# RWKV-7 waves: alpha and key-times-a kept in DRAM, y normalised on ScalarE, two steps of the scores' order exchanged

## The chip, the cores and the metric

The kernel runs on one core of a Trainium2 chip. The metric is the time of one execution on the device in microseconds (us). The engines are named as in the profile: PE is TensorE (PEld its weight loads), DVE is VectorE, ACT is ScalarE, POOL is GpSimd, SP is SyncE, which here issues every DMA.

## The reference

One inference step of a two-layer trunk, layer 0 gated DeltaNet, layer 1 RWKV-7, on 1024 + 16 prompt rows and 8 sequences of 8 sample rows, 1024 wide. Only the RWKV layer is touched. Per head (16 heads of 64) and per row t it computes, with the vectors r, k, v, the decay d and the gate a:

```python
kk = l2norm((k * k_k).reshape(B, T, H, N))
k = k * (1.0 + (a - 1.0) * k_a)
decay = jnp.exp(-jnp.exp(w))
b_h = kk * a_h
def step(S, inp):
    S = (S * d_t[:, :, None, :]
         + jnp.einsum('bhvk,bhk->bhv', S, -kk_t)[..., None] * b_t[:, :, None, :]
         + v_t[..., None] * k_t[:, :, None, :])
    return S, jnp.einsum('bhvk,bhk->bhv', S, r_t)
...
y = (y - mean) * lax.rsqrt(var + GN_EPS) * lnx_w.reshape(H, N) + lnx_b.reshape(H, N)
y = y + jnp.sum(r_h * k_h * r_k, -1, keepdims=True) * v_h
y = y.reshape(B, T, D) * jax.nn.silu(z)
return y @ w_o, S, xn[:, -1]
```

## The kernel before

The rows are cut into three segments of 384, 384 and 336 and the heads into eight pairs, so there are 24 tiles "pair of heads x segment" of [128 features, 384 rows]. Each tile has six chunks of 64 rows. The kernel computes the recurrence in its chunked form: alpha is kk times the decay up to the row before, the keys times a are divided by the decay (kk * a * iD), and inside a chunk the rank-one updates need the inverse of a triangular matrix.

The RWKV layer has three stages. First the projections for k, with decay and a (`keys_decay_rate`), which write their results to DRAM (`csd`, `kd`, `ad`). Second the projections for r, v and part of the gate z. Between these, `rwkv_inverse` works through the 24 tiles in five groups: `rwkv_keys` makes kk, Dp (decay) and iD (its inverse), `alpha` makes the alpha tile `sal`, two products make the tile kk * a * iD, PE multiplies them, and the inverses go to DRAM as `ttd`. Third `wave`: it walks through 58 waves (tau from -3 to 54). A tile takes two waves to enter, six waves to run through its chunks, and is finished some waves later; three tiles are in flight at a time. In this stage the order on PE is as written in the program (`manual_schedule`); the other engines' queues, and all of them before this stage, are ordered by the framework's scheduler, which simulates the program. Blocks under `high_priority` go first there, and `issue_after` keeps a wave's other work behind its inner step.

In a wave `step_solve` multiplies the scores G with the ring UV (values above, solved rows below) and the alpha half of AR with the state; ACT copies the result to X; `step_inner` multiplies with the inverse TT; ACT writes the solved rows back into UV; then fillers run (output projections, the gate), and `step_state` updates states and y. Around this, for each tile:

- `rwkv_front` loads cs, k, a, r and v from DRAM, and makes kk, Dp, iD, AR (alpha and r times decay), k2 and BK (the two keys over the decay). It makes alpha and kk * a * iD a second time, on POOL.
- Six parts follow in two waves, three in each, as `P.parts` lists them: `scores(0)` and `scores(3)` (each takes both PSUM banks of the tag "f", which DVE empties into G), `bonus`, `values` (three transposes; ACT copies them into the ring), `keys(0)` and `keys(3)` (three transposes each; ACT copies them into BT), and `system` (the load of TT). A wave runs its first part between solve and inner step, its second before `step_state`, its third after it.
- `rwkv_finish` takes mean and variance of y on DVE, the power on POOL, three steps of refinement on DVE, and normalises six tiles of 128x64 on POOL (L1551); PE transposes them in a later wave, and the bonus and the gate follow.

## Time and profile before

| | |
|---|---|
| median of 3 runs | 2374.34 us (2370.59 to 2375.54) |
| profiled execution | 2374.91 us, its span 2373.2 us |
| instructions | 54463 |
| first and last inner step of the waves | 1876.0 and 2327.2 us after the span's start |
| mean granted PE clock | 0.967 |

Lines of the profile give a start in us, a duration in us, engine, line, operation and tiles; a bracket holds the idle time of that engine just before, and what ended it. "x6" counts merged instructions. A group's row has busy us and mean ns of one instruction, then the idle time before.

### The profile page before, as it was taken

The numbers are of one execution on the slowest core, as the hardware profiler recorded it, in microseconds if no ns is written. First come the engines' busy times: TensorE is split into PE (matmuls) and PEld (weight loads), VectorE is DVE, ScalarE is ACT, GpSimd is POOL, SyncE is SP. The second block draws the span as 40 slices with busy tenths as digits, with TensorE's granted clock in tenths as the row PEclk, the third lists the DMA queues.
The fourth block names the chain that finished last, engine by engine and source line by source line (L and its number), as shares of the span: only waits on it lengthen the run. The fifth ranks groups of instructions, "written<-read, shape, count | busy, mean of one in ns | idle before, by whom it ended". The sixth has DMA issues, their size and how long they took to land. (4 is left out here: it accounts for less than half of the span.)

```text
span 2373.2 us, 54463 instructions
## 1 busy us (share of the span) xinstructions
PE 2168.7 (91%) x19737; PEld 1962.9 (83%) x19737; DVE 1617.0 (68%) x4195; ACT 1248.0 (53%) x3479; POOL 1113.8 (47%) x1566
## 2 busy tenths in 40 slices
PE   5989999999999999999989998998999888888886
PEld 5888989888898989898989998987878776777775
DVE  6868677685858686873346724389896666778754
ACT  5455655554656555566243646555453454556552
POOL 3435343343444353433223513355454666777764
PEclk9999999999999999999999999999999999999998
DMA  3323332324233333435262245566754544555543
GB/s 113 106 74 104 87 102 78 96 71 113 68 105 94 85 98 88 115 107 163 62 165 76 72 156 173 143 164 165 188 135 129 178 115 141 158 178 182 178 138 125
DMA packets 470535, 290.01 MB, mean 122 GB/s; under 512 B 188121, under 2 KB 455642, under 8 KB 470266
## 3 DMA queue, kind: packets, MB, share of 16 engines
q1 hardware_dynamic: 470266, 286.53, 42.7%
q8 instruction: 156, 2.56, 0.5%
q14 instruction: 113, 0.93, 0.1%
HBM read 200.53 MB, written 85.89 MB: 121 GB/s over the span
## 5 line engine op out<-in xcount | busy, mean ns | idle before, releaser
L90 POOL TENSOR_TENSOR wlo<-wraw,whi 128x512 fp32r<-128x512 f32 (+2 forms) x252 | 329.7, 1311 | 349.2 <-ACT whi L86 323.2
L76 PE MATMUL d<-xc,whi 128*128 128x384 f32 (+2 forms) x910 | 259.1, 341 | 4.8 <-POOL xc L90 2.8
L86 ACT CAST whi<-wraw 128x512 fp32r<-128x512 f32 (+2 forms) x252 | 151.6, 603 | 130.6 <-PE dq L76 50.5
L419 DVE SCALAR_TENSOR_TENSOR cvy<-raw,cw,cvy 128x408 f32<-128x408 f32 (+2 forms) x288 | 178.9, 634 | 17.6 <-ACT cvy L62 15.7
L452 DVE TENSOR_TENSOR invtmp<-invA,invT 72x31 f32<-72x31 f32 (+31 forms) x403 | 170.4, 423 | 13.0 <-DMA invA<-ltd 5.1
L76 PEld LDWEIGHTS d<-xc,whi 128*128 128x128 f32 (+1 forms) x910 | 167.8, 191 | 12.6 <-issue 5.3
L454 DVE TENSOR_TENSOR invT<-invT,invtmp 72x31 f32<-72x31 f32 (+31 forms) x403 | 168.9, 419 | 6.7
L76 PE MATMUL dz<-xc,whi 128*128 128x384 f32 (+1 forms) x480 | 148.3, 340 | 0.0
L76 PE MATMUL dv<-xc,whi 128*128 128x384 f32 (+1 forms) x480 | 146.8, 335 | 0.0
L76 PE MATMUL d<-xc,wlo 128*128 128x384 f32 (+2 forms) x428 | 142.7, 342 | 0.0
L76 PE MATMUL d<-xa,whi 128*128 128x384 f32 (+3 forms) x450 | 139.0, 344 | 3.3 <-DVE xa L90 1.7
L868 POOL TENSOR_SCALAR Sb<-Sb,eglb 128x128 f32<-128x128 f32 x128 | 81.3, 651 | 88.1 <-DMA Sb<-in_state_gdn 23.7
L1551 POOL TENSOR_SCALAR y<-y,mv,grs 128x64 f32<-128x64 f32 x144 | 83.8, 599 | 42.8 <-DVE grs L106 40.0
L76 PE MATMUL dv<-xa,whi 128*128 128x384 f32 (+1 forms) x288 | 99.9, 347 | 0.1
L76 PE MATMUL dz<-xa,whi 128*128 128x384 f32 (+1 forms) x288 | 99.5, 346 | 0.0
L76 PEld LDWEIGHTS d<-xa,whi 128*128 128x128 f32 (+1 forms) x450 | 84.3, 192 | 9.7 <-issue 3.3
L76 PEld LDWEIGHTS dz<-xc,whi 128*128 128x128 f32 x480 | 88.9, 191 | 0.8
L76 PEld LDWEIGHTS dv<-xc,whi 128*128 128x128 f32 x480 | 88.5, 188 | 0.5 <-issue 0.4
L76 PE MATMUL d<-xh,wlo 128*128 128x384 f32 (+1 forms) x256 | 85.2, 348 | 1.6 <-POOL wlo L90 1.6
L76 PE MATMUL d<-xa,wlo 128*128 128x384 f32 (+3 forms) x252 | 86.4, 343 | 0.0
L76 PE MATMUL d<-xh,whi 128*128 128x384 f32 (+1 forms) x256 | 84.5, 344 | 0.5 <-ACT whi L86 0.5
L76 PE MATMUL d<-xl,whi 128*128 128x384 f32 (+1 forms) x256 | 84.5, 347 | 0.0
(514 smaller groups left out, 7171.7 us busy)
## 6 DMA issues: line engine op xcount, KB each, us to landing
wraw<-in_gdn_w_in SPq DMA_DIRECT2D x96, 256.0 KB
wraw<-in_rwkv_w_rkvz SPq DMA_DIRECT2D x80, 256.0 KB
Sb<-in_state_gdn SPq DMA_DIRECT2D x64, 256.0 KB
wraw<-in_rwkv_w_o SPq DMA_DIRECT2D x40, 256.0 KB
E<-drow SPq DMA_DIRECT2D x24, 384.0 KB
attn<-drow SPq DMA_DIRECT2D x24, 384.0 KB
wraw<-in_gdn_w_out SPq DMA_DIRECT2D x36, 256.0 KB
out_s_gdn<-Sb SPq DMA_DIRECT2D x32, 256.0 KB
```

The source lines that it names most:

```text
L76: self.nc.tensor.matmul(out, lhsT, rhs, start=start, stop=stop)
L86: nc.scalar.copy(hi, x)
L90: e.tensor_tensor(lo, x, hi.bitcast(F32), op=ALU.subtract)
L419: nc.vector.scalar_tensor_tensor(y[:, 0:wd], raw[:, k:k + wd], cw[k], y[:, 0:wd], op0=ALU.mult, op1=ALU.add)
L452: nc.vector.tensor_tensor(tmp, A[:, j, j + 1:32].unsqueeze(2).broadcast_to([nb, n, m]), Tv[:, j, 0:m].unsqueeze(1).broadcast_to([nb, n, m] ...
L454: nc.vector.tensor_tensor(Tv[:, j + 1:32, 0:m], Tv[:, j + 1:32, 0:m], tmp, op=ALU.subtract)
L868: nc.gpsimd.tensor_scalar(Sb[:, u], Sb[:, u], self.eglb[:, hv, 4 * g + u:4 * g + u + 1], None, op0=ALU.mult)
L1551: nc.gpsimd.tensor_scalar(y(q), y(q), mv[:, q, 0:1], rs[:, q:q + 1], op0=ALU.subtract, op1=ALU.mult)
```

## The change

It has three parts. (1) The inverse stage writes each tile's alpha and kk * a * iD to two DRAM tensors, `ald` and `bkd`; the front reads them into AR and BK instead of computing them, so its kk (ACT), the alpha product and its one or two small copies, and the two products on POOL fall away. AR's layout becomes [128, 2, 6, 64], so that alpha is one run of 384 in a row of AR and r times decay another; the matmuls that read AR index it accordingly. The read for BK fills six pieces of 64 elements a row. (2) The normalisation of y is an ACT activation with a scale and a bias for each of the six tiles; the bias, minus mean times scale, is one more DVE instruction of 128x6. (3) In the order of parts `keys(0)` takes the place of `values`, and `values` stands with `system`, where `keys(0)` stood.

```diff
+        self.ttd, self.ald, self.bkd = (self.dram([24, 128, 384], n) for n in ("ttd", "ald", "bkd"))
...
-        kk = t(pool, [128, 384], tag + "kk", 2 if tag == "s" else 1)
+        kk = t(pool, [128, 384], tag + "kk", 2)
...
             nc.vector.tensor_tensor(kk, kk, iD, op=ALU.mult)
+            nc.sync.dma_start(self.ald[n], al.rearrange("p c k -> p (c k)"))
+            nc.sync.dma_start(self.bkd[n], kk)
...
-        kk, Dp, iD = self.rwkv_keys(p, ld, fp, "f")
+        Dp, iD = self.rwkv_decays(ld, fp, "f")
...
-        AR = P.AR = t(fp, [128, 6, 2, 64], "AR", NB + 1)
+        AR = P.AR = t(fp, [128, 2, 6, 64], "AR", NB + 1)
+        BK = t(fp, [128, 6, 2, 64], "BK", 2)
+        nc.sync.dma_start(AR[:, 0].rearrange("p c k -> p (c k)"), self.ald[P.n])
+        nc.sync.dma_start(BK[:, :, 1, :], self.bkd[P.n].rearrange("p (c k) -> p c k", k=64))
-        self.alpha(AR[:, :, 0, :], kk, Dp, s, nc.gpsimd)
-        nc.vector.tensor_tensor(AR[:, :, 1, :], c6(ld["r"]), c6(Dp[:, 1:385]), op=ALU.mult)
+        nc.vector.tensor_tensor(AR[:, 1], c6(ld["r"]), c6(Dp[:, 1:385]), op=ALU.mult)
...
-        nc.gpsimd.tensor_tensor(kk, kk, ld["a"], op=ALU.mult)
-        BK = t(fp, [128, 6, 2, 64], "BK", 2)
         nc.vector.tensor_tensor(BK[:, :, 0, :], c6(k2), c6(iD), op=ALU.mult)
-        nc.gpsimd.tensor_tensor(BK[:, :, 1, :], c6(kk), c6(iD), op=ALU.mult)
...
-                    self.mm(gp[h][:, 128 * u:128 * u + 128], flat(BK[q, c + u]), flat(AR[q, c + u]))
+                    self.mm(gp[h][:, 128 * u:128 * u + 128], flat(BK[q, c + u]), AR[q, :, c + u])
...
-        P.parts = [[lambda: scores(0)], [bonus], [values], [lambda: scores(3)], [system, lambda: keys(0)], [lambda: keys(3)]]
+        P.parts = [[lambda: scores(0)], [bonus], [lambda: keys(0)], [lambda: scores(3)], [system, values], [lambda: keys(3)]]
...
         self.rsqrt(rs, va, ap, "gn")
+        nm = t(ap, [128, 6], "gnm", 2)
+        nc.vector.scalar_tensor_tensor(nm, mv[:, :, 0], -1.0, rs, op0=ALU.mult, op1=ALU.mult)
         for q in range(6):
-            nc.gpsimd.tensor_scalar(y(q), y(q), mv[:, q, 0:1], rs[:, q:q + 1], op0=ALU.subtract, op1=ALU.mult)
+            self.act(y(q), y(q), AF.Identity, scale=rs[:, q:q + 1], bias=nm[:, q:q + 1])
```

The two other readers of AR (`step_solve`, `rwkv_sample_read`) change their index order only, and `rwkv_decays` is the part of `rwkv_keys` that makes Dp and iD.

More of the change, by code (lines that the diff above doesn't have):

```diff
@@ L1251, in rwkv_open @@
                                                                  ("csd", "ad", "rd", "vd", "zd", "kd"))
-        self.ttd = self.dram([24, 128, 384], "ttd")
+        self.ttd, self.ald, self.bkd = (self.dram([24, 128, 384], n) for n in ("ttd", "ald", "bkd"))
     def rwkv_load(self, n, pool, tag, names):
@@ L1267, in rwkv_keys, with rwkv_decays @@
         nc, t = self.nc, self.t
-        kk = t(pool, [128, 384], tag + "kk", 2 if tag == "s" else 1)
+        kk = t(pool, [128, 384], tag + "kk", 2)
         self.act(kk, ld["k"], AF.Identity, scale=self.pcol["rwkv_k_k"][:, p:p + 1])
+        return kk, *self.rwkv_decays(ld, pool, tag)
+    def rwkv_decays(self, ld, pool, tag):
+        nc, t = self.nc, self.t
         Dp, iD = t(pool, [128, 385], tag + "Dp", 1), t(pool, [128, 384], tag + "iD", 1)
@@ L1273, in rwkv_keys @@
         self.act(iD, ld["cs"], AF.Exp, scale=self.DEC)
-        return kk, Dp, iD
+        return Dp, iD
     def alpha(self, al, kk, Dp, s, eng):
@@ L1473, in step_solve @@
                     for h in (0, 1):
-                        self.mmw(W, name, (h + x) % 2, 64 * q, P.AR[hs[h], ci, x], S[hs[h]])
+                        self.mmw(W, name, (h + x) % 2, 64 * q, P.AR[hs[h], x, ci], S[hs[h]])
         nc = self.nc
@@ L1591, in rwkv_sample_read @@
                 a = 64 * h
-                self.mm(rp[a:a + 64, 16 * b:16 * b + 16], P.Sb[a:a + 64, b, :], AR[a:a + 64, 0, :, 8 * b:8 * b + 8])
+                self.mm(rp[a:a + 64, 16 * b:16 * b + 16], P.Sb[a:a + 64, b, :], AR[a:a + 64, :, 0, 8 * b:8 * b + 8])
         q = t(ap, [128, 2, 8, 8], "rkst", 1)
```

## Prediction

> **What bounds the kernel now.** I read the page first (engines and slices), then the busy time of stretches inside the last fifth, then what TensorE (PE) waited for there, and last the timelines of single waves. PE is the busiest engine overall, and in the wave part of the RWKV layer, which the change mostly touches, it is the engine that sets the end: its order is written out by hand, so each of its waits there is time lost.
>
> ```profile
> PE 2168.7 (91%) x19737; PEld 1962.9 (83%) x19737; DVE 1617.0 (68%) x4195; ACT 1248.0 (53%) x3479; POOL 1113.8 (47%) x1566
> ```
>
> The four stretches below are four waves in a row. Odd waves (the second half of a pair's scores) alternate with even ones; the columns are busy time by engine, granted clock, DMA share. The last row is the steady part with 14 pairs.
>
> ```profile
> 2105.80:2116.70 10.90, 8.86 (x127) 7.61 (x126) 7.89 (x25) 4.00 (x11) 6.28 (x8) 0.84 0.66 212
> 2116.70:2123.80 7.10, 6.88 (x103) 5.83 (x101) 5.59 (x11) 5.83 (x17) 7.04 (x11) 1.00 0.38 108
> 2123.80:2133.20 9.40, 7.49 (x129) 6.32 (x128) 7.78 (x25) 4.00 (x11) 6.29 (x8) 1.00 0.77 249
> ...
> 2020.00:2273.00 253.00, 221.35 (x3321) 186.48 (x3321) 198.20 (x537) 144.02 (x399) 191.40 (x245) 0.95 0.56 172
> ```
>
> An even wave has PE busy for 6.88 of 7.10 us: nothing to gain. An odd one leaves it idle for 1.9 of 9.40. PE's waits name the cause, first in the steady part, then in the earlier part with the sample rows (1876 to 2020):
>
> ```profile
> PE fBT L73 <- DVE G L1393: 25.1, 14, 2.1
> ```
> ```profile
> PE fG L76 <- ACT UV L1415: 4.8, 6, 1.4
> ```
>
> So 25.1 of the 31.65 us that PE idles in the steady part (253.00 less 221.35) is one wait: the first key transposes need a PSUM bank of the tag "f", which has two, and both hold the scores' second half until VectorE (DVE) has multiplied it into G. In one odd wave PE finishes its filler and stands:
>
> ```profile
> 2125.30 0.34 PE L76 MATMUL do<-yh,wlo 128*128 128x384 f32 x1
> 2127.55 0.55 PE L73 MATMUL fBT<-ident,BK 128*128 128x128 f32 x3 [1.91 <-DVE G L1393]
> ```
>
> DVE is late because the next pair's front work stands ahead of G in its queue:
>
> ```profile
> 2120.61 2.03 DVE L1354 TENSOR_TENSOR AR<-fldr,fDp 128x384 f32<-128x384 f32 x1 [0.27 <-ACT fDp L62]
> ...
> 2123.03 1.04 DVE L1357 TENSOR_TENSOR k<-k,fldk 128x384 f32<-128x384 f32 x1
> ...
> 2124.25 1.37 DVE L1361 TENSOR_TENSOR BK<-k,fiD 128x384 f32<-128x384 f32 x1
> 2125.55 1.34 DVE L1367 SCALAR_TENSOR_TENSOR pr<-fldr,pcol,k 128x384 f32<-128x384 f32 x1
> ...
> 2126.97 0.98 DVE L1393 TENSOR_TENSOR G<-fG,gm 128x384 f32<-128x384 f32 x2
> ```
>
> and each of those is slow because GpSimd (POOL) works at the same moment:
>
> ```profile
> 2116.62 3.39 POOL L1551 TENSOR_SCALAR y<-y,mv,grs 128x64 f32<-128x64 f32 x6 [2.42 <-DVE grs L106]
> 2119.98 1.02 POOL L90 TENSOR_TENSOR yl<-lz,yh 128x384 fp32r<-128x384 f32 x1
> 2120.95 1.27 POOL L90 TENSOR_TENSOR wlo<-wraw,whi 128x512 fp32r<-128x512 f32 x1
> ...
> 2122.66 0.99 POOL L1280 TENSOR_TENSOR AR<-fkk,fDp 128x384 f32<-128x384 f32 x1
> ...
> 2124.20 1.01 POOL L1358 TENSOR_TENSOR fkk<-fkk,flda 128x384 f32<-128x384 f32 x1
> 2125.29 1.19 POOL L1362 TENSOR_TENSOR BK<-fkk,fiD 128x384 f32<-128x384 f32 x1
> ```
>
> The same shapes alone on DVE take a half: the alpha product of the inverse stage (min/median/max ns), and a three-operand one of the waves (mean ns, third column from the end).
>
> ```profile
> L1280 DVE TENSOR_TENSOR sal<-skk,sDp x24: 544/552/1649, 1476.6 to 1738.7; 128x384 f32<-128x384 f32 x24
> ```
> ```profile
> L1560 DVE SCALAR_TENSOR_TENSOR lz<-k,lnb,lz 128x384 f32<-128x384 f32 x16 | 9.9, 619 | 0.0
> ```
>
> **Term 1, the wait for G.** The change takes four kinds of POOL work out: AR, kk, BK (0.99 + 1.01 + 1.19) from the odd wave, the six y (3.39) from the even one. k, BK and pr on DVE lose their partners and should fall to 0.55, 0.55 and 0.62, which saves 0.49 + 0.82 + 0.72 = 2.03 us ahead of G. AR keeps yl and wlo as neighbours, but these start about 0.85 us earlier once y no longer stands before yl; I take nothing for it as the lower bound and 0.85 as the upper. So G comes 2.0 to 2.9 us earlier against a wait of 1.91 here and 2.1 at most. The bank rotation itself stays: the value transposes now stand where the key transposes stood, behind both halves of the scores, and inherit the wait; it goes because DVE is early, not because the order changed. I leave 1.1 us in all for what remains: 24 us saved (bounds 0 and 25.1).
>
> **Term 2, the clock.** The waves at 2105.80 and 2123.80 hold the same work; the first, at a granted clock of 0.84, is 1.5 us longer, with PE busy 8.86 against 7.49. Over the steady part 0.95 granted means some 5% of 253 us, 12.6 us lost. The slow wave is one with the same G wait as the fast one, so a wait is not enough for a drop; but with the waits most should go. I take a half, 6 us (bounds 0 and 12.6). The Trainium skill (TensorE: Matmul & The Clock Gate, "Why this matters for your kernels") states that the clock falls after a window of about 3 us or more without matmuls; no PE wait in the row above is that long and the clock still fell, so here the trace goes further than the rule. By the rule the drops would not come from these waits, and term 2 would be 0, the sum 6 us smaller.
>
> **Term 3, the sample part.** There the scores' second half waits for ScalarE (ACT) to empty the bank of the value transposes, two to four copies in a chain; the key transposes that come in their place need one. Rows of both, from one pair:
>
> ```profile
> 2119.55 0.61 ACT L62 ACTIVATE fkk<-fldk,pcol 128x384 f32<-128x384 f32 x1
> ...
> 2121.83 1.07 ACT L1415 COPY UV<-fVT 64x256 f32<-64x256 f32 x4
> ...
> 2128.13 0.48 ACT L1402 COPY BT<-fBT 128x384 f32<-128x384 f32 x1
> ...
> 2132.41 0.32 ACT L1483 COPY X<-rX 128x192 f32<-128x192 f32 x1 [1.37 <-PE rX L80]
> 2133.76 0.33 ACT L62 ACTIVATE UV<-rX 64x192 f32<-64x192 f32 x1 [1.04 <-PE rS L80]
> ...
> 2134.34 0.83 ACT L62 ACTIVATE pre<-rS,DC 128x64 f32<-128x64 f32 x3
> ```
>
> 1.07 against 0.48 is about a half of the 4.8 us: 3 saved (0 to 4.8).
>
> **Term 4, more work on ACT.** Six normalisations of 128x64 at the price of "pre", 0.83 / 3 = 0.28, are 1.66 us a pair. The even wave, where ACT is busy for 5.83 of 7.10, loses fkk (0.61) and the value copies (1.07) and gains one BT copy (0.48) and the 1.66: 0.46 more, 6.29 of 7.10. The value copies go to the odd wave, where ACT is busy for 4.00 of 9.40, and must end before the next wave's first product; the 5 us that it has then fit. The extra product on DVE (128x6) is hidden in its idle time. The scores' matmuls now read AR as two runs of 64; no row prices that, I take nothing. What hides the 0.46 is the idle time before X and UV (1.37 and 1.04); without that cover it costs 0.46 x 23 = 10.6. I take 3 us lost (0 to 10.6).
>
> **Term 5, the transfers.** 24 pairs write two tiles of 192 KB in the inverse stage and read them back in the waves, 96 more issues on the one queue (SP). Shares of the queue in the two stretches, 1475 to 1750 and 2020 to 2273 (packets, MB, share of 16 engines), the price of an issue (ns), a late landing from the chain, the issue of the load that fkk at 2119.55 reads, and the reuse of the alpha tile in the inverse stage, which has one buffer:
>
> ```profile
> q1 hardware_dynamic: 95338, 44.36, 62.3%
> ```
> ```profile
> q1 hardware_dynamic: 42768, 43.01, 55.4%
> ```
> ```profile
> L1318 SPq DMA_DIRECT2D rltd<-sgl x24: 367/383/1269, 1501.5 to 1747.7; - x24
> ```
> ```profile
> 2311.77 3.33 DMA wraw<-in_rwkv_w_o
> ```
> ```profile
> 2106.17 0.45 SPq L1262 DMA_DIRECT2D fldk<-kd  x1
> ```
> ```profile
> 1508.14 0.56 DVE L1280 TENSOR_TENSOR sal<-skk,sDp 128x384 f32<-128x384 f32 x1 [4.84 <-PE fL L76]
> ...
> 1516.22 0.57 DVE L1280 TENSOR_TENSOR sal<-skk,sDp 128x384 f32<-128x384 f32 x1 [4.55 <-PE fL L76]
> ```
>
> The first stretch gives 28.8 ns of engine time a packet at a mean 465 B, the second 52.4 ns at 1006 B: a line of 8.5 ns + 0.0437 ns a byte, so 76 ns for a row of 1536 B and 20 for a piece of 256 B. Estimate: 48 x 128 x 76 / 16 = 29 us of the queue's time in the inverse stage (its share goes from 62% to 73%), and 24 x (128 x 76 + 768 x 20) / 16 = 38 us in the waves, about 8 points. There is room in both. The Trainium skill (DMA: Bandwidth & Descriptors, "Specifications") asks for at least 512 B a piece for full rate, and the beta read is cut into pieces of 256 B. No run here shows a piece of that size by itself; if each cost what my line gives for 512 B, 31 ns, a read would take 1.5 us of the queue instead of 1.0. An alpha tile is written back after its two small POOL copies (I allow 1 us after 1508.14), must have landed (3.33 at the worst seen) before 1516.22, and does by some 3 us. The skk tile has two buffers. What is queued behind: on SP a weight load or the inverse's small transfers wait up to 0.38 us an issue, and an issue that waits for its data holds them longer. All issues on PE's path in the inverse stage would be 48 x 0.38 = 18 us. I take 4 us lost (0 to 18), near the low end since PE hardly waits for transfers there. In the waves the two reads need no work of the same pair; like the load of k, issued 13 us before its use, they can go a wave ahead.
>
> **Term 6, the end.** After the last wave POOL's six y stand before the last weight splits, on the chain that ended last:
>
> ```profile
> 2335.55 0.56 POOL y L1551
> ```
>
> On ACT, which is idle then, they end sooner: 3.39 - 1.66 = 1.7, about 2 saved (0 to 2.3). Sum: -24 - 6 - 3 + 3 + 4 - 2 = -28 us. The profiled execution took 2374.91 us (span 2373.2), 0.6 above the median of the runs, so it needs no correction: 2347 us.
>
> **Rival A, slower: ACT stands behind the normalisation's scale.** The y work waits for POOL's power and three DVE steps. POOL could afford this; on ACT the copies X and UV of the wave queue behind.
>
> ```profile
> POOL y L1551 <- DVE grs L106: 40.0, 23, 3.9
> ```
> ```profile
> 2130.07 1.35 POOL L103 TENSOR_TENSOR grs<-va,cvals 128x6 f32<-128x6 f32 x1 [0.26 <-DVE va L1548]
> ```
> ```profile
> 2131.41 0.62 DVE L1559 SCALAR_TENSOR_TENSOR k<-fyT,lnw,rbv 128x384 f32<-128x384 f32 x1 [0.49 <-PE fyT L76]
> 2131.95 0.15 DVE L104 TENSOR_TENSOR gn_t<-grs 128x6 f32<-128x6 f32 x1
> ```
>
> If the scheduler puts all six ahead of X, ACT waits 40.0 and works 23 x 1.66 = 38, less 23 x 1.37 = 31 of idle time there: 47 us on the chain, against the 31 that terms 1 to 3 and 6 bring beyond term 5: 2374.9 - 31 + 47 = 2391. It decides from a loss of 31 / 23 = 1.3 us a pair. Against it: the order on DVE puts gn_t behind a step that itself waited 0.49 for PE; a scheduler that took the power for short would have put it before. It seems to know that the scale is late, and would place y after X. Chance 0.13.
>
> **Rival B, a smaller gain:** DVE stays blocked by yl, wlo and the bonus split, and G comes only 1 us earlier; half of term 1 and none of term 2 are left: 12 + 3 + 2 - 7 = 10 saved, 2365. For it: AR's neighbours remain. Against: the three others' leave. The Trainium skill (SBUF — State Buffer, "SBUF: two separate sides") makes the pair's port an exclusive lock held for a whole instruction; a DVE step that meets wlo would then wait up to its full 1.27 us, and AR here spans just the rest of yl and all of wlo. Chance 0.20.
>
> **Rival C, nothing gained:** the reads of alpha and beta come late on the queue, and the first scores wait for them; 1.2 us a pair (the wait for G was 25.1 / 14 = 1.8) make 24 x 1.2 = 28 us: 2375. Against: five and two buffers, a wave of lead. Chance 0.05.
>
> **How the numbers follow.** Forecast 0.62 at 2347; A 0.13, B 0.20, C 0.05. Its own bounds: with all of terms 1, 2, 3 and 6 and no cost, 2374.9 - 44.8 = 2330; the range starts at 2333 and reaches to C at 2374, and leaves out A and a little at the fast end. 0.2% is about 5 us, what a measurement of this kernel can tell from no change. Faster by more: forecast and B, 0.82; within: C, 0.05; slower: A, 0.13.
>
> **What would show it.** Right: PE's wait for G in 2020 to 2273 below 5 us and odd waves near 7.5 us; AR below 1.5 us, k, BK and pr near 0.6; a granted clock above 0.95; the time up to the first wave longer by at most 5 us. Wrong: PE waiting for X or UV from ACT with y just ahead (A); the value transposes waiting for G by more than 1 us (B); scores waiting for a transfer of ald or bkd (C); or an inverse stage that grows by more than 10 us.

## The result, and the profile after

The change makes the kernel faster by 0.5%, where 1.2% was forecast: median 2363.89 us (7 runs, 2360.66 to 2371.43) against 2375.54 for the kernel before in the same comparison (7 runs, 2370.59 to 2384.93), ratio 0.9953, 95% interval 0.9936 to 0.9971. In microseconds that is 11 saved, 7 to 15 by the interval, instead of 28. In a later comparison, with other kernels below, the same kernel came out at 0.9928 (0.9909 to 0.9948), 17 us saved, 12 to 22; both fall short of the forecast. The profiled executions stand at 2362.64 and 2374.91 us, spans 2360.9 and 2373.2.

The first thing to read is the same cut of the waves in both kernels. The boundaries are inner steps of the same waves: the first one, tau 17 (the last sample rows are in), tau 44 (no new tile enters), tau 51, the end of the span. Between them lie the sample part, the steady stage, the drain and the end. Columns: length, busy time of PE, PEld, DVE, ACT, POOL, granted clock, DMA share, GB/s. Before, the stretch from the first alpha product of the inverse stage to the first inner step, then the four wave stages:

```profile
1476.60:1876.00 399.40, 366.17 (x3416) 325.42 (x3415) 294.59 (x596) 199.43 (x430) 197.13 (x277) 0.92 0.61 159
1876.00:2039.00 163.00, 138.76 (x1922) 113.61 (x1921) 109.80 (x317) 82.64 (x223) 110.42 (x142) 0.93 0.45 130
2039.00:2273.00 234.00, 204.28 (x3105) 172.88 (x3104) 184.66 (x500) 135.18 (x377) 179.96 (x230) 0.96 0.57 174
2273.00:2327.20 54.20, 46.58 (x631) 39.38 (x629) 25.39 (x102) 26.23 (x82) 34.60 (x45) 0.97 0.55 164
2327.20:2373.20 46.00, 26.37 (x182) 22.24 (x182) 19.92 (x53) 11.33 (x33) 17.66 (x26) 0.85 0.29 94
```

After:

```profile
1476.90:1882.80 405.90, 368.21 (x3417) 326.63 (x3415) 290.88 (x597) 198.61 (x428) 193.21 (x267) 0.93 0.66 177
1882.80:2048.30 165.50, 138.61 (x1922) 111.67 (x1921) 101.38 (x323) 89.48 (x249) 55.86 (x66) 0.92 0.56 160
2048.30:2258.90 210.60, 194.59 (x3104) 166.70 (x3103) 148.29 (x512) 153.62 (x443) 91.38 (x96) 1.00 0.72 217
2258.90:2316.10 57.20, 49.04 (x629) 41.13 (x627) 25.82 (x105) 33.65 (x105) 21.17 (x20) 0.91 0.54 163
2316.10:2360.90 44.80, 26.19 (x182) 22.12 (x182) 19.82 (x57) 13.87 (x41) 14.80 (x21) 0.83 0.29 92
```

The steady stage is 23.4 us shorter and PE runs there at the full clock (1.00 granted). Of this, 11 us are given back: 6.5 ahead of the first wave, 2.5 in the sample part, 3.0 in the drain (where the clock stood at 0.91 instead of 0.97), while the end gains 1.2. So most of the forecast sum arrived in one stage, and the question is why the others gave some of it back.

PE's waits in the steady stage of after (total us, times, longest):

```profile
PE rS L80 <- ACT UV L62: 9.2, 10, 1.1
PE rX L80 <- DMA rTT<-ttd: 2.4, 2, 1.3
```

The transposes' wait for G, 25.1 us before (23.2 of it in this stage), is gone from the list. The largest wait is now a new one: the last product of the solve (`rS`) waits for ACT to write the solved rows into the ring. The two waves below, odd and even, show both sides: the odd wave fell from 9.40 to 7.20 us with PE busy throughout, the even one rose from 7.10 to 7.90.

```profile
2109.40:2116.60 7.20, 7.20 (x127) 6.33 (x126) 5.28 (x22) 4.36 (x12) 3.56 (x3) 1.00 0.90 286
2116.60:2124.50 7.90, 6.95 (x103) 5.85 (x101) 5.31 (x16) 6.75 (x19) 3.16 (x4) 1.00 0.63 173
```

What happens in that even wave is on ACT's timeline, with PE's step that waits:

```profile
2115.84 0.32 ACT L1489 COPY X<-rX 128x192 f32<-128x192 f32 x1 [1.37 <-PE rX L80]
...
2116.99 2.10 ACT L62 ACTIVATE y<-y,gnm,grs 128x64 f32<-128x64 f32 x6 [0.83 <-DVE gnm L1557]
2119.11 0.33 ACT L62 ACTIVATE UV<-rX 64x192 f32<-64x192 f32 x1
```
```profile
2119.71 0.57 PE L80 MATMUL rS<-UV,BT 128*64 128x64 f32 x12 [0.94 <-ACT UV L62]
```

ACT copies X, stands 0.83 us for the bias of y, does all six y in 2.10 us, and only then writes UV, 3.27 us after X began. Before, X began at 2132.41 and UV at 2133.76, 1.35 us later (both rows are quoted in the prediction). PE loses 0.94 us by it.

The steps ahead of G on DVE did what was forecast, except one (groups of the steady stage: busy us, mean ns | idle before; the first row is AR in the kernel before, the others are of after):

```profile
L1354 DVE TENSOR_TENSOR AR<-fldr,fDp 128x384 f32<-128x384 f32 x13 | 25.0, 1920 | 2.7 <-ACT fDp L62 2.6
```
```profile
L1363 DVE TENSOR_TENSOR AR<-fldr,fDp 128x384 f32<-128x384 f32 x13 | 10.5, 808 | 9.0 <-ACT fDp L62 9.0
L1366 DVE TENSOR_TENSOR k<-k,fldk 128x384 f32<-128x384 f32 x13 | 11.8, 908 | 0.0
L1368 DVE TENSOR_TENSOR BK<-k,fiD 128x384 f32<-128x384 f32 x13 | 6.9, 534 | 0.0
L1373 DVE SCALAR_TENSOR_TENSOR pr<-fldr,pcol,k 128x384 f32<-128x384 f32 x14 | 8.5, 605 | 0.0
```

BK and pr have the price of the undisturbed rows and AR is down from 1920 ns. Only k stays slow: where it starts at 2107.77 it runs beside POOL's split of a weight tile (2106.83 to 2108.45) and its copy of DC.

### The profile page after: what moved, and what is told of

Read it like the earlier page. It is cut to its first block, busy times and chain, and to the rows that moved or that the text cites. A ratio compares the mean times of both kernels' runs of the same rounds, so it can differ in the third digit from the quotient of the medians.

```text
span 2360.9 us, 54503 instructions
## 1 busy us (share of the span) xinstructions
PE 2167.1 (92%) x19737; PEld 1961.9 (83%) x19737; DVE 1571.2 (67%) x4219; ACT 1282.6 (54%) x3599; POOL 949.4 (40%) x1318
## 5 line engine op out<-in xcount | busy, mean ns | idle before, releaser
L419 DVE SCALAR_TENSOR_TENSOR cvy<-raw,cw,cvy 128x408 f32<-128x408 f32 (+2 forms) x288 | 178.3, 632 | 15.7 <-ACT cvy L62 13.8
L62 ACT ACTIVATE o<-rA,gcol 128x128 f32<-128x128 f32 x128 | 46.6, 372 | 72.6 <-DVE S L779 72.0
L76 PEld LDWEIGHTS d<-xc,wlo 128*128 128x128 f32 (+1 forms) x428 | 82.1, 194 | 4.0 <-issue 1.9
```

The lines of the kernel that those rows point to most:

```text
L62: return self.nc.scalar.activation(out, in_, func, bias=bias, scale=scale, **kw)
L76: self.nc.tensor.matmul(out, lhsT, rhs, start=start, stop=stop)
L419: nc.vector.scalar_tensor_tensor(y[:, 0:wd], raw[:, k:k + wd], cw[k], y[:, 0:wd], op0=ALU.mult, op1=ALU.add)
```

## The experiments

Each part of the change was run alone and with the others; then stalls that came to light were taken away. "Full change" is the kernel after; M is the DRAM part, Y the normalisation on ACT, P the order of the parts, "split" three of the six normalisations on ACT and three on POOL, "ue" and "TT" four buffers where there are two and three, of the tiles of that tag in the sample rows' state update and of the loaded inverse (`rTT`). Ratios are to the kernel before in the same comparison; comparisons are numbered. The stages are those of the profiled executions, cut as above (clock in brackets); "waves" is from the first inner step to the end of the span, even / odd the median lengths of the steady waves, all worked out from the starts of the inner steps.

| kernel | no. | ratio (95%) | first wave at | waves | sample | steady | even / odd |
|---|---|---|---|---|---|---|---|
| before | | 1 | 1876.0 | 497.2 | 163.0 | 234.0 (0.96) | 7.10 / 9.41 |
| full change | 1 | 0.9953 (0.9936–0.9971) | 1882.8 | 478.1 | 165.5 | 210.6 (1.00) | 8.01 / 7.22 |
| M | 2 | 0.9882 (0.9848–0.9916) | 1896.8 | 469.7 | 159.4 | 209.2 (0.99) | 7.34 / 7.34 |
| Y | 2 | 0.9969 (0.9946–0.9991) | 1883.3 | 496.5 | 166.5 | 229.1 (0.97) | 8.67 / 8.49 |
| P | 2 | 1.0046 (1.0020–1.0072) | 1878.9 | 510.4 | 162.8 | 247.4 (0.91) | 6.50 / 11.42 |
| M+P | 2 | 0.9883 (0.9854–0.9912) | 1883.4 | 475.4 | 161.3 | 210.8 (0.97) | 6.95 / 7.75 |
| writes only | 3 | 1.0028 (1.0006–1.0050) | 1879.2 | 493.7 | 159.9 | 233.5 (0.96) | 7.09 / 9.41 |
| M+Y | 3 | 0.9964 (0.9945–0.9983) | 1878.1 | 482.2 | 166.1 | 214.7 (0.99) | 8.27 / 7.21 |
| full + ue | 3 | 0.9886 (0.9854–0.9918) | 1884.4 | 459.4 | 148.8 | 210.6 (1.00) | 8.02 / 7.22 |
| M+P + ue | 3 | 0.9897 (0.9869–0.9926) | 1880.7 | 467.2 | 151.8 | 215.2 (0.96) | 7.25 / 7.51 |
| before + ue | 4 | 0.9941 (0.9921–0.9962) | 1878.2 | 485.4 | 148.1 | 233.9 (0.96) | 7.11 / 9.47 |
| M + ue + TT | 4 | 0.9860 (0.9832–0.9889) | 1880.3 | 460.5 | 152.2 | 206.8 (0.98) | 6.75 / 7.73 |
| full + ue, y a wave later | 4 | 0.9938 (0.9909–0.9966) | 1885.3 | 476.4 | 157.8 | 217.0 (1.00) | 7.55 / 8.78 |
| the same + TT | 4 | 0.9915 (0.9890–0.9940) | 1887.7 | 471.5 | 154.9 | 216.8 (1.00) | 7.55 / 8.78 |
| full change | 5 | 0.9928 (0.9909–0.9948) | 1877.8 | 477.9 | 166.9 | 211.3 (1.00) | 8.02 / 7.22 |
| M | 5 | 0.9907 (0.9889–0.9925) | 1886.9 | 474.7 | 159.1 | 211.7 (0.98) | 7.32 / 7.34 |
| full, y behind UV | 5 | 0.9992 (0.9977–1.0007) | 1881.2 | 491.6 | 172.0 | 220.7 (0.97) | 8.08 / 7.24 |
| full, split | 5 | 0.9879 (0.9860–0.9899) | 1882.2 | 472.1 | 162.9 | 204.4 (0.99) | 7.31 / 7.22 |
| full + ue + TT | 6 | 0.9871 (0.9844–0.9898) | 1891.3 | 462.1 | 149.5 | 210.8 (1.00) | 8.02 / 7.22 |
| split + ue + TT | 6 | 0.9801 (0.9772–0.9829) | 1884.7 | 453.9 | 153.5 | 201.8 (0.99) | 7.06 / 7.23 |

Four warnings on it. Between comparisons the kernel before itself had medians from 2375.5 to 2383.4 us, so kernels are compared first within one; M and the full change each ran in two. The time to the first wave scatters by several us for identical work ahead of it: the first alpha product starts at 1490.8 in M's first profile, at 1476.6 in that of before. The sample part scatters too: "writes only" runs the same waves as the kernel before, and took 159.9 us there against 163.0. And the drain (not in the table) follows the clock: 53 to 55 us at 0.97, 57 to 59 at 0.91, in kernels with and without each part.

**The DRAM part alone (M).** The normalisation back on POOL, the old order.

```diff
-        P.parts = [[lambda: scores(0)], [bonus], [lambda: keys(0)], [lambda: scores(3)], [system, values], [lambda: keys(3)]]
+        P.parts = [[lambda: scores(0)], [bonus], [values], [lambda: scores(3)], [system, lambda: keys(0)], [lambda: keys(3)]]
...
-            self.act(y(q), y(q), AF.Identity, scale=rs[:, q:q + 1], bias=nm[:, q:q + 1])
+            nc.gpsimd.tensor_scalar(y(q), y(q), mv[:, q, 0:1], rs[:, q:q + 1], op0=ALU.subtract, op1=ALU.mult)
```

> The changed kernel with y on POOL and the old order of parts, so only the DRAM part. My theory: the key transposes' wait for G is under 5 us, even waves at 7.1 us, odd ones at 7.2 to 7.6; the stages before the first wave still about 7 us longer than before; 2350 to 2358 us. Rival (the order matters too): 10 us or more of the wait for G stay and the time is 2362 to 2375.

Measured: 2360.50 us, 0.9882 (0.9848 to 0.9916), and 27.5 us less in the waves. PE's waits in its steady stage:

```profile
PE rX L80 <- DMA rTT<-ttd: 8.0, 7, 4.0
PE dfin L73 <- DVE f2k L1691: 2.5, 1, 2.5
PE fBT L73 <- DVE G L1399: 1.5, 3, 0.7
```

The wait for G is down to 1.5 us with the key transposes where they always stood. So it was DVE's lateness and not the order that made it, and this part alone brings the gain. Its new cost is the load of the inverse (`rTT`), which now comes late: 8.0 us in seven waits. The even waves, 7.34 us, are a little longer than the 7.1 expected, and the time lies just above the range.

**The normalisation alone (Y)** and **the order alone (P)**, each put into the kernel before.

```diff
+        nm = t(ap, [128, 6], "gnm", 2)
+        nc.vector.scalar_tensor_tensor(nm, mv[:, :, 0], -1.0, rs, op0=ALU.mult, op1=ALU.mult)
-            nc.gpsimd.tensor_scalar(y(q), y(q), mv[:, q, 0:1], rs[:, q:q + 1], op0=ALU.subtract, op1=ALU.mult)
+            self.act(y(q), y(q), AF.Identity, scale=rs[:, q:q + 1], bias=nm[:, q:q + 1])
```

> The kernel before with only y on ACT. My theory: most of the wait for G stays (k, BK and pr still meet POOL's three products), 12 to 25 us, and the even waves gain about 1 us of waiting for UV each: 2372 to 2388 us. Rival (y on POOL was the cause): the wait for G falls under 5 us and the time to 2350 to 2362.

```diff
-        P.parts = [[lambda: scores(0)], [bonus], [values], [lambda: scores(3)], [system, lambda: keys(0)], [lambda: keys(3)]]
+        P.parts = [[lambda: scores(0)], [bonus], [lambda: keys(0)], [lambda: scores(3)], [system, values], [lambda: keys(3)]]
```

> The kernel before with only the new order of parts. My theory: the bank rotation is the same, so the value transposes now wait for G, 20 to 28 us in the steady waves; the wait of the scores' second half for ACT in the sample part falls by 1 to 3 us; time 2370 to 2377 us. Rival (the order removed the wait): wait under 5 us, time 2345 to 2358.

Measured: Y 2378.12 us, 0.9969 (0.9946 to 0.9991); P 2391.93 us, 1.0046 (1.0020 to 1.0072). PE's waits in the steady stage, Y first, then P:

```profile
PE fG L76 <- ACT UV L1415: 12.4, 13, 1.9
PE rS L80 <- ACT UV L62: 7.3, 12, 0.8
PE fBT L73 <- DVE G L1393: 4.6, 4, 1.3
```
```profile
PE fVT L73 <- DVE G L1393: 30.1, 13, 2.7
```

Y alone also takes most of the wait for G away (23.2 to 4.6), which I had not seen: I had expected 12 to 25 us to stay, so its time, which lies in my range, came out right by luck. Without the six y, POOL is out of the way of DVE's steps sooner, and the row of AR, 1920 ns a step in the kernel before, becomes

```profile
L1354 DVE TENSOR_TENSOR AR<-fldr,fDp 128x384 f32<-128x384 f32 x13 | 15.7, 1208 | 4.0 <-ACT fDp L62 4.0
```

But it hands the time back at once on ACT: 12.4 us before the scores' second half, which needs the bank of the value copies, and 7.3 us at `rS`. The even wave grows by 1.57 us while the odd one falls by 0.92. P alone shows that the bank rotation carries the wait over to whoever stands there: now the value transposes wait, 30.1 us, more than the 20 to 28 expected, the clock of the stage falls to 0.910, and the kernel is slower than before, outside the range. P by itself gains nothing.

**All but the normalisation (M+P).** The change with y back on POOL, the second edit of M's diff.

> The changed kernel with y back on POOL (DRAM part and order kept). My theory: the wait for G left because the front's products left POOL, so it stays away here (under 5 us in the steady waves), and the even waves' new wait of the state products for UV from ACT (10.1 us in the changed kernel) goes, as y no longer stands ahead of UV: 2350 to 2356 us. Rival: the six y leaving POOL were what brought DVE forward; then 10 to 25 us of the wait for G come back and the time is 2362 to 2375.

Measured: 2359.44 us, 0.9883 (0.9854 to 0.9912): the same as M in the same comparison, some 3 us above my range; the wait for G stays away as expected (3.4 us) and no wait of `rS` for UV is left. The order is worth nothing that the ratios can tell, once DVE is early.

**The other way round (M+Y):** the change with the old order, the first edit of M's diff.

> The changed kernel with the old order of parts (DRAM part and y on ACT kept). My theory: the order of parts is worth little once DVE is early; the wait for G stays under 5 us, the even waves keep their wait for UV; 2360 to 2368 us. Rival (the order matters): 10 us or more of the wait for G come back, or the value copies ahead of X in the even waves add to the wait for ACT; 2370 to 2380.

Measured: 2369.38 us, 0.9964 (0.9945 to 0.9983), the waves 482.2 us against M's 469.7: 6.7 of the difference in the sample part, 5.5 in the steady one. Even waves are 0.93 us longer than M's. PE's two largest waits in the steady stage are `rS` for UV, 6.5 us, and the scores' second half for the value copies, 6.4 us, which was one branch of the rival. So the loss comes with Y, and the old order doesn't take it away; its size across comparisons is left to the runs beside one another below.

**The writes alone.** The kernel before, with the 48 writes of the inverse stage into tensors that nobody reads.

```diff
+        self.ald, self.bkd = (self.dram([24, 128, 384], n) for n in ("ald", "bkd"))
...
+            nc.sync.dma_start(self.ald[n], al.rearrange("p c k -> p (c k)"))
+            nc.sync.dma_start(self.bkd[n], kk)
```

> The kernel before, with the inverse stage also writing the two tensors (48 transfers of 192 KB); nothing reads them. It prices the writes. My theory: they are what makes the stages before the first wave longer: the first inner step comes 4 to 9 us later than before (1876.0 us), the waves are unchanged, 2378 to 2384 us. Rival: the delay comes from another order of the queues (the reads, the freed buffers); then the first inner step moves by less than 2 us and the time is 2373 to 2378.

Measured: 2383.32 us, 1.0028 (1.0006 to 1.0050), some 7 us by the ratio (1 to 12). Its profile shows 3.2 us more ahead of the first wave and 3.5 less in the waves, but the profiled execution, 2374.64 us, is the fastest of the ten and can't show where the 7 us went. From the first alpha product to the first inner step, before, Y and P took 399.4 to 402.5 us, and M, M+P, M+Y and the full change with and without more buffers 400.3 to 407.1: two or three us, which the 6.5 us of the first pair overstates. With the writes alone it took 400.7, only 1.2 us more. Which step of the stage loses them stays open.

**The sample part: four buffers for `ue`.** There PE's largest waits in the profile of after have little to do with the scores. `drsw` is the product that updates the sample rows' states; its input tile and the tile from which the new states are written out share the two buffers of the tag `ue`. The kernel before first, then after:

```profile
PE drsw L76 <- DVE xss L1603: 9.2, 6, 2.5
```
```profile
PE drsw L76 <- DVE xss L1611: 15.7, 5, 4.7
PE drsw L76 <- DVE bnst L1551: 5.0, 2, 2.9
PE fG L76 <- ACT BT L1408: 2.6, 3, 1.4
```

One of the five, followed back: PE waits for DVE, DVE for a buffer that the write of the sample states (`out_s_rwkv`) still reads, and that write goes out in blocks of eight issues on SP:

```profile
1912.85 1.97 PE L76 MATMUL drsw<-ue,BT 128*64 128x512 f32 x4 [4.69 <-DVE xss L1611]
```
```profile
1911.42 0.69 DVE L1618 TENSOR_TENSOR ue<-UV,bmask 128x512 f32<-128x512 f32 x1 [4.62 <-DMA out_s_rwkv<-ue]
```
```profile
1903.86 5.92 SPq L1636 DMA_DIRECT2D out_s_rwkv<-ue  x8
```

The wait was there before (DVE for that DMA, before and after):

```profile
DVE ue L1610 <- DMA out_s_rwkv<-ue: 19.0, 6, 4.5
```
```profile
DVE ue L1618 <- DMA out_s_rwkv<-ue: 24.1, 7, 6.0
```

Four buffers instead of two, in the full change, in M+P, and in the kernel before:

```diff
-        ue = [t(self.fin, [128, 8, 64], "ue", 2) for h in (0, 1)]
+        ue = [t(self.fin, [128, 8, 64], "ue", 4) for h in (0, 1)]
...
-        so = t(self.fin, [128, 4, 2, 64], "ue", 2)
+        so = t(self.fin, [128, 4, 2, 64], "ue", 4)
```

> The changed kernel with four buffers instead of two for the tile ue of the sample rows. My theory: in the sample part DVE stands until the written-out state has left its buffer (ue waits 24.1 us for out_s_rwkv), and TensorE with it (drsw, 20.7 us); the extra issues on SP made this worse. With four buffers DVE's wait falls below 6 us, the sample part gets 10 to 16 us shorter, and the time is 2347 to 2355. Rival: the transfers of the sample state are limited by SP's issue time itself, and the wait moves to another tile of that chain; the sample part gains under 4 us and the time is 2359 to 2366.

> The changed kernel with y back on POOL and four buffers for ue. My theory: both gains add up, 2336 to 2346 us. Rival: they meet in the same waves and only the larger is kept, 2347 to 2355.

> The kernel before with four buffers for ue instead of two. It asks whether the sample part was bound by that tile already before the change. My theory: yes; DVE's wait for out_s_rwkv (19.0 us) was there, and TensorE's drsw wait (9.2 us) goes; the sample part (163.0 us from the first to the 18th inner step) gets 6 to 12 us shorter, the time 2362 to 2370. Rival: before the change other waits of that part (G, fG for the value copies, zz) stand ready to take its place, and it gains under 4 us: 2371 to 2377.

Measured: the full change 2348.24 us, 0.9886 (0.9854 to 0.9918), sample part 148.8 us instead of 165.5; M+P 2351.89, 0.9897 (0.9869 to 0.9926), sample part 151.8 instead of 161.3; the kernel before 2368.08, 0.9941 (0.9921 to 0.9962), sample part 148.1 instead of 163.0. The wait of `drsw` is down to 2.7 us in the sample part of the full change, and a wait of the product `zz` for DVE now leads:

```profile
PE zz L76 <- DVE zst L1037: 4.9, 1, 4.9
PE fG L76 <- ACT BT L1408: 3.8, 5, 1.1
PE drsw L76 <- DVE xss L1611: 2.7, 6, 0.5
```

In all three kernels, the one before included, four buffers shorten the sample part by 9.5 to 16.7 us, so two buffers held it back in each. The steady stage of the full change stays as it was, 210.6 us, with the wait of `rS` for UV at 9.5 us. M+P with four buffers lies in the rival's range: its two gains don't add up in full. Here the kernel with Y was no slower than the one without (2348.24 against 2351.89), which the last pair below takes up again.

**The normalisation a wave later.** If y between X and UV is the steady stage's loss, moving it to the odd wave, where ACT has room, should bring the even wave back. On top of the four buffers, the six activations are emitted behind the inner step and `pre` of wave 2n + 7:

```diff
+        yield
         for q in range(6):
             self.act(y(q), y(q), AF.Identity, scale=rs[:, q:q + 1], bias=nm[:, q:q + 1])
...
+                if tau % 2 and 0 <= (tau - 7) // 2 < 24:
+                    next(P[(tau - 7) // 2].done)
```

> The changed kernel with four buffers for ue, and the six activations of y issued two waves later in the program's order, in the odd wave in which their transposes come (ACT is busy there for 4.5 of 7.2 us). My theory: what the even waves lost (8.0 against 7.1 us, PE's rS waiting for UV, 9.5 us) is y standing ahead of UV on ACT; the wait falls under 3 us, even waves to 7.0 to 7.3 us, odd ones stay under 7.6, the steady part (210.6) falls to 198 to 204, the time to 2336 to 2344. Rival: ACT is simply too full (the place in the queue doesn't matter); the wait moves to the odd waves and the steady part stays at 207 or more, 2345 to 2352.

Measured: 2363.46 us, 0.9938 (0.9909 to 0.9966), slower than the rival had it too, where the place in the even wave had given 0.9886 in another comparison. The wait of `rS` is gone and even waves fall to 7.55 us, but odd ones rise to 8.78. The new wait, PE's largest, and its place:

```profile
PE fyT L76 <- ACT UV L1421: 18.4, 13, 1.5
```
```profile
2122.98 2.09 ACT L62 ACTIVATE y<-y,gnm,grs 128x64 f32<-128x64 f32 x6
...
2126.01 1.07 ACT L1421 COPY UV<-fVT 64x256 f32<-64x256 f32 x4
```
```profile
2127.14 0.92 PE L76 MATMUL fyT<-ident,y 64*64 64x64 f32 x24 [1.50 <-ACT UV L1421]
```

The 2 us on ACT push the value copies back, and the transposes of y need the bank that these empty. ACT is busy for 6.3 us of these odd waves, so here it is not full; a place behind the value copies was not tried.

**A fourth buffer for the inverse.** The new wait for `rTT` is taken away by loading it earlier: four tiles in turn instead of three, with M and the four `ue` buffers, and once more with the later normalisation.

```diff
-        self.TTz = [t(ap, [128, 6, 64], f"rTT{q}") for q in range(3)]
+        self.TTz = [t(ap, [128, 6, 64], f"rTT{q}") for q in range(4)]
```

> Only the DRAM part (y on POOL, old order of parts) with four buffers for ue and four instead of three for TT. My theory: the DRAM part alone is what gains; the inner step's waits for the load of TT (8.0 us there) go, since the load no longer has to wait for the wave that used the buffer; the wave stages together (469.7 us with the DRAM part alone, 459.4 in the changed kernel with four ue) take 445 to 455 us, the time is 2332 to 2343. Rival: TT is late because SP is late, not because of its buffer; the wait stays at 5 us or more, 2344 to 2352.

> The y_later kernel with four buffers for TT too: all parts of the change kept. My theory: about 2 us less than y_later, as its waits for TT are few (1.5 us in the kernel with four ue): 2334 to 2343, within 4 us of the DRAM part alone with the same buffers. Rival: the new order of parts and y on ACT still cost, 5 us or more above the DRAM part alone.

Measured: M with both 2347.13 us, 0.9860 (0.9832 to 0.9889), with no wait for `rTT` left in the steady stage. That part of the theory held, but the waves took 460.5 us instead of 445 to 455, and the time lies in the rival's range. The load is now issued 10 to 27 us ahead of its first use in the steady stage, where M issued it 1 to 9 us and the kernel before 4 to 11 us ahead. Whether the third buffer or the place on the queue had held it back is not told apart. The later normalisation 2360.96, 0.9915 (0.9890 to 0.9940), in the same comparison: the move still costs, as the rival of that run had it. In M's steady stage POOL does y again and AR on DVE is slow again, and that costs PE next to nothing (its two largest waits):

```profile
L1363 DVE TENSOR_TENSOR AR<-fldr,fDp 128x384 f32<-128x384 f32 x13 | 28.4, 2183 | 0.0
```
```profile
PE fG L76 <- DVE k L1565: 4.5, 1, 4.5
PE fBT L73 <- DVE G L1399: 2.6, 5, 0.6
```

**Size and cause of Y's loss, side by side.** What was open: by different comparisons Y cost anything from nothing to 20 us, and it was not told apart whether by its place ahead of UV, by the wait for its bias, or by its time on ACT. Four kernels on one chip: the full change and M as they were,

> The changed kernel itself, unaltered, beside the DRAM part alone in the same comparison. The theory (the normalisation on ACT takes back more than half of what the DRAM part gains): ratio near 0.995 to the kernel before, and at least 8 us above the DRAM part alone. The rival (the gap between the two was a matter of different comparisons, in which the kernel before itself had medians of 2375.5 and 2382.9): the two within 5 us of each other.

> The DRAM part alone (y on POOL, the old order), unaltered. The theory: 2355 to 2361 us, ratio 0.988 to 0.991, waves near 470 us. The rival: as slow as the full change, 2362 to 2366.

the full change with y emitted in the even wave behind the inner step, so that ACT has it behind UV and `pre`,

```diff
+        yield
         for q in range(6):
             self.act(y(q), y(q), AF.Identity, scale=rs[:, q:q + 1], bias=nm[:, q:q + 1])
...
                     self.step_old(W)
+                if tau % 2 == 0 and 0 <= (tau - 6) // 2 < 24:
+                    next(P[(tau - 6) // 2].done)
```

> The full change, with the six normalisations emitted in the even wave behind its inner step, so that on ACT they stand behind the two ring writes UV and the three of pre instead of ahead of them. The theory (the loss in the steady stage is their place ahead of UV): PE's wait of rS for UV, 9.2 us, goes below 2; even waves fall from 8.0 to near 7.3 us; the steady stage falls below 206 us at the full clock, and the total by 5 to 9 us. The rival (the two microseconds on ACT are lost wherever they stand): another wait of 6 us or more takes its place, most likely of the next X or of the y transposes, and the total stays within 4 us of the full change.

and the full change with three of the six on each engine:

```diff
         for q in range(6):
-            self.act(y(q), y(q), AF.Identity, scale=rs[:, q:q + 1], bias=nm[:, q:q + 1])
+            if q < 3:
+                self.act(y(q), y(q), AF.Identity, scale=rs[:, q:q + 1], bias=nm[:, q:q + 1])
+            else:
+                nc.gpsimd.tensor_scalar(y(q), y(q), mv[:, q, 0:1], rs[:, q:q + 1], op0=ALU.subtract, op1=ALU.mult)
```

> The full change, with three of a pair's six normalisations on ACT and three on POOL. The theory (loss by time on ACT ahead of UV): ACT holds UV for about 1.05 us less, so the rS wait goes nearly to nothing (it was 0.94 us in a wave) and the total is 4 to 9 us below the full change. The rival (what costs is the wait for the scale and bias, 0.83 us, which stays): even waves fall by less than 0.3 us and the total by less than 3.

Measured: the full change 2364.15 us, 0.9928 (0.9909 to 0.9948); M 2358.45, 0.9907 (0.9889 to 0.9925), 5.7 us less by the medians but with overlapping intervals; y behind UV 2378.68, 0.9992 (0.9977 to 1.0007); the split 2351.20, 0.9879 (0.9860 to 0.9899), 13 us below the full change, intervals apart, which is more than the 4 to 9 expected. Against M the split is 7 us faster, with overlapping intervals.

The expectation of more than 8 us between the full change and M was too high. The theory of the place fell too: behind UV the wait of `rS` is indeed gone, but the even wave is as long as in the full change (8.08 us), another wait has come, and the total, 14.5 us above the full change, is worse than the rival had it. The sample part is 5.1 us longer and the steady stage 9.4; of the latter some 7 are the clock by an estimate (0.969 granted instead of 1.000 over 220.7 us). ACT's even wave and PE's largest wait in all waves:

```profile
2110.60 0.83 ACT L62 ACTIVATE pre<-rS,DC 128x64 f32<-128x64 f32 x3
2111.34 2.09 ACT L62 ACTIVATE y<-y,gnm,grs 128x64 f32<-128x64 f32 x6
...
2116.02 0.48 ACT L1408 COPY BT<-fBT 128x384 f32<-128x384 f32 x1
```
```profile
PE fG L76 <- ACT BT L1408: 19.6, 15, 2.2
```

From y on ACT works without a pause, the key copies (BT) come last, and the next scores wait for their bank. So in the even wave it is the amount: six on ACT in one pair are about a microsecond more than it can take, and of the two places there each only chose who waits. The split fits. It leaves the wait for the bias as it was (0.87 us), and behind UV y doesn't wait for its bias and the loss stays, so the bias isn't the cause by itself; ahead of UV its wait and the work add up, and an earlier bias was not tried:

```profile
2111.76 1.11 ACT L62 ACTIVATE y<-y,gnm,grs 128x64 f32<-128x64 f32 x3 [0.87 <-DVE gnm L1557]
2112.89 0.33 ACT L62 ACTIVATE UV<-rX 64x192 f32<-64x192 f32 x1
```

Even waves fall to 7.31 us, the steady stage to 204.4, and the wait of `rS` for UV leaves the list; what leads it now is the load of the inverse:

```profile
PE rX L80 <- DMA rTT<-ttd: 6.3, 5, 1.9
```

**The same pair without the other two stalls:** six on ACT against the split, both with four `ue` and four inverse buffers.

> The full change with four buffers for ue and for the inverse, all six normalisations on ACT. Theory (the three losses are separate: two buffers of ue in the sample part, three of the inverse, six normalisations ahead of UV): about what the four ue buffers alone gave, ratio 0.986 to 0.989, with PE's wait of rS for UV still near 9 us in the steady stage. Rival (with the sample chain gone the normalisation's loss is covered): as fast as the version with the split, within 3 us.

> The same with three normalisations on ACT and three on POOL. Theory: no rS wait, no rTT wait, even and odd waves near 7.2 us, 6 to 10 us below the other kernel of this comparison, ratio 0.982 to 0.985, the fastest version. Rival: within 3 us of it.

Measured: six on ACT 2348.93 us, 0.9871 (0.9844 to 0.9898); the split 2335.04, 0.9801 (0.9772 to 0.9829), the fastest kernel here. The 14 us between them are about the same as with the stalls in place. In the profiles 9.0 of them are in the steady stage (210.8 and 201.8) and 6.6 ahead of the first wave, where both kernels do the same work; the sample part is 4.0 us longer with the split. PE's largest waits in the steady stage, six on ACT first:

```profile
PE rS L80 <- ACT UV L62: 10.5, 12, 1.1
```
```profile
PE fG L76 <- DVE k L1570: 2.9, 1, 2.9
```

## Why the prediction was right or wrong, by its own steps

The step that failed is term 4, the normalisation on ACT. It stood in the sum with +3 us, within 0 to 10.6. In the steady stage alone PE's new wait behind it measures 9.2 us (8.5 to 10.5 in three more profiles with six on ACT), and with only three on ACT that stage is 6.9 and 9.0 us shorter. By the medians the two pairs differ by 13 and 14 us; in the first, 4.0 us more are in the sample part, and the rest the profiles don't locate. This is the price of six against three. Against none it isn't settled: M, with all six on POOL, was 5.7 us faster side by side, with overlapping intervals, and M+P with four `ue` was no faster than the full change with them.

Term 3's sign comes on top, and then smaller pieces. The profiles of before and after differ by 12.3 us where the sum said 28. The shortfall of 15.7 is 3.6 in the steady stage (23.4 saved, terms 1, 2 and 4 said 27), 5.5 in the sample part, 2.8 ahead of the first wave (6.8 later, term 5 said 4), 3.0 in the drain and 0.8 at the end. With the split the change measures 29 us saved (0.9879; 24 to 33). That this is the size of the forecast is luck: term 3 is still missing in it.

**Term 4** failed in its price and in its cover. The row of the group, busy us and mean ns of one:

```profile
L62 ACT ACTIVATE y<-y,gnm,grs 128x64 f32<-128x64 f32 x78 | 27.3, 428 | 11.5 <-DVE gnm L1557 11.5
```

One record lasts 428 ns, and six in a row overlap to 350 each: 2.10 us a pair, not 1.66. I had taken "pre", which has a scale column only. The Trainium skill (ScalarE: Activation LUTs, "What ACT_TABLE_LOAD costs") gives 186 ns plus 0.833 ns an element, 93 ns for each operand that is a column, and an overlap of 93 ns between neighbours; an estimate by these figures is 425 ns for one and 2.09 us for six, which the trace bears out. So ACT is busy for 6.75 us of the even wave instead of 6.29, and the idle time before X and UV that I named as cover can't be used: y waits for its bias until after X has begun, and of the 2.93 us of wait and work only 1.04 were idle before. The upper bound, 0.46 a pair, was the excess of work alone; measured, six against three, are 0.7 to 1.0 us of an even wave (8.02 against 7.31 and 7.06).

**Term 1** was right: the 25.1 us that the transposes waited for G became no row at all in the steady stage of after, 1.5 in M, with BK and pr near their undisturbed price (k stays at 0.91 in after and is at 0.58 in M). AR gained 1.1 us, more than the 0.85 that I had as its upper bound. That the order would not be what removes it was right too (P: 30.1 us). Not seen was that two parts would each do most of it alone.

**Term 2**, the clock, was right in sign and size: 0.964 to 1.000 over 210.6 us is 7.6 us of the stage, against 6. By the rule of the Trainium skill weighed there (TensorE: Matmul & The Clock Gate, "Why this matters for your kernels") the drops would have had to stay, since no wait for G reached 3 us; they went with the waits of 2 us, and P's waits of up to 2.7 us came with a clock of 0.910. But in the drain of the first profiled pair it fell from 0.97 to 0.91, some 3 us back; the second profile of the same kernel had 0.97 and a drain of 54.6 us there, so that part is scatter.

**Term 3** named the wrong bound. Its wait did fall, 4.8 to 2.6 us, and yet the sample part grew by 2.5 us (3.9 in the second profile of after): the transfer of sample states out of two buffers held it back, and the row for that (19.0 us on DVE, 9.2 on PE) stood in the profile of before. I had read PE's waits for the change's own tiles there, not the list's first row. The growth itself goes with term 4: with two `ue` buffers the kernels with all six on ACT took 165.5 to 172.0 us in that part, the others 159.1 to 163.0.

**Term 5** can't be told from its size: 7 us (1 to 12) for the writes by themselves by the ratio, 1 to 3 in the profiles of the inverse stage, against 4. The queue's share between 1475 and 1750 us came to 70.4% where 73% was worked out. What I left out is the load of `rTT`, for which PE now waits 2.4 us in after and 8.0 in M. No wait of PE for the reads of alpha and beta shows in any kernel, so **rival C** is out, and the size of the pieces played no part that a wait of PE shows.

**Term 6** brought 1.2 us of the 2.

**Rival A**'s mechanism is the one that came, in a smaller form: y stood ahead of UV instead of ahead of X, and the loss stayed below the 1.3 us a pair from which it decides. **Rival B** gave 2365 us, within 2 of the result, but by luck, for a reason that the traces exclude: G was early and hardly any wait for it was left.

## What to carry to other kernels

Work moved to an engine with idle time is paid for when the stretch it lands in is nearly full: add up that engine's busy time for the very wave, at the price of the very form of instruction, and ask which copy each place in the queue delays. In the three places tried here the wait only changed its name; dividing the work between two engines was worth 13 us. Before pricing a step in a stage, read the first row of that stage's waits, whether or not it touches your change: two more buffers for a state write, put into the kernel before, were worth about as much as the whole edit aimed at all waves (0.9941 against 0.9953 and 0.9928). And run a change of several parts one part at a time, side by side.

## What the runs showed of the hardware that was not expected

- The clock's drops come in fixed portions. In the steady stage of before it was lowered five times, each time to 0.50 for 3.4 us. All changes of the granted clock in a trace lie on one grid of 3.41 us, and in before PE was busy for 38 to 50% of the stretch just ahead of each drop (1.37 of 3.41 us from 2106.59, then 0.51 granted until 2113.41), while stretches with 55% or more passed without one. A wait of 1.92 us that fell into one stretch (until 2058.86) lowered the clock; one of 1.91 us that lay across a grid line (until 2076.74, the line at 2075.8) did not. Neither the longest wait nor this share decides everywhere: with y behind UV no wait passed 1.5 us and the stage had 0.969 (one drop followed 2.01 busy of 3.40 us), and with y a wave later it had 1.00 with thirteen waits of up to 1.5 us. What else counts stays open.
- A normalisation with both a scale and a bias column took 428 ns for a tile of 128x64, 350 each in a row of six.
- AR on DVE ranged from 808 to 2183 ns (means of a steady stage) for the same product, the slow ones where POOL worked on y, and the slowest stood in a kernel with 2.6 us of waiting for G: being slow is not yet being late.
